# A two-layer hybrid decoder trunk: recurrence levels on 64-column halves, and low halves of 30 weight blocks of each mixer added by a DMA

## The chip, the cores and the metric

The kernel runs on one core of one Trainium2 chip. The metric is device time in microseconds (us) of one execution; the kernel before took 2127.11 us, the median of 3 runs (2126.46 to 2127.39). A profile is one execution with the hardware profiler on. Its engines: PE is TensorE's matmul side and PEld its weight load, DVE is VectorE, ACT is ScalarE, POOL is GpSimd, SP is SyncE, which here only issues DMAs.

## What is computed

Two layers, each with a half-step gated feed-forward, a mixer, and a second feed-forward; 512 tokens, width 1024, all in float32. The change lies in the mixer's gated linear recurrence (4 heads, 128 x 128 state, chunks of 64 tokens in the reference) and in how the mixer's weights are prepared.

```python
for l in range(DEPTH):
    h = rms_norm(x, gn[0])
    x = x + 0.5 * rms_norm(swiglu(h, w_ffn1_gate[l], w_ffn1_up[l], w_ffn1_down[l]), gn[1])
    h = rms_norm(x, gn[2])
    proj = h @ w_in[l]
    hq, hf, hi, hg, aq, ak, av, gate_a, gate_b = jnp.split(proj, IN_SPLITS, axis=-1)
    y_hg = hgrn2_mixer(hq, hf, hi, hg, lb_all[l], hgrn_head_gain[l]) @ w_branch_hgrn[l]
    y_at = swa_sink_attention(aq, ak, av, attn_sinks[l]) @ w_branch_attn[l]
    mixed = jax.nn.sigmoid(gate_a) * y_hg + jax.nn.sigmoid(gate_b) * y_at
    x = x + rms_norm(mixed @ w_out[l], gn[3])
    h = rms_norm(x, gn[4])
    x = x + 0.5 * rms_norm(swiglu(h, w_ffn2_gate[l], w_ffn2_up[l], w_ffn2_down[l]), gn[5])
...
# in hgrn2_mixer, per chunk
G = jnp.cumsum(gb, axis=2)
diff = G[:, :, :, None, :] - G[:, :, None, :, :]
decay = jnp.exp(jnp.where(causal[:, :, None], diff, -jnp.inf))
scores = jnp.einsum('bhtd,bhtsd,bhsd->bhts', qb, decay, kb)
o = o_inter + jnp.einsum('bhts,bhse->bhte', scores, vb)
```

A score of the recurrence between a query t and an earlier key s is the sum over d of q[t,d], k[s,d] and the product of the forget gates f between them. The kernel needs those scores for the whole sequence of 512 tokens.

## The kernel before

**Weights.** Every large product is made of three products of float32r halves: high by high, high by low, low by high. A `Stream` brings the weights in blocks of 128 x 1024 through four buffers `w`, issued on SP's queue. `Stream.split` makes a block's halves: ScalarE casts the block to `whi` (L321), and then one of two ways makes `wlo`. For kind "u" VectorE subtracts (L328). For kinds "v", "a" and "d" ScalarE writes the negated rounded block to `wlo` (L325) and a DMA issued on POOL's queue adds the block into it (L326). Six slots hold `whi` and `wlo`; blocks are split three ahead of the one in use, and as far as the slots allow. A slot is free when TensorE has used the block, 24 products of 512 columns.

**Order on TensorE.** The program writes TensorE's order out by hand. `mm` adds each product's estimated time to a clock, `order.t`. Coroutines (recurrence heads, attention blocks) run in steps; each step ends with a `yield` of a time after which the next is due, taken from the table WAIT. After each block of a weight product `order.poll` runs the steps that are due, so their products are put between the large ones. The other engines' order is chosen by the framework.

**Recurrence scores** (`recurrence_scores`, once for each of 4 heads in each of 2 layers). `kz`, `q`, `f` are 128 x 512: the head's 128 channels by 512 tokens, four tiles of 128 tokens. The levels b = 1, 2, 4, 8, 16, 32, 64 join neighbouring blocks of b tokens to blocks of 2b. At each level the odd block's queries times the even block's keys give scores, with `qa` and `kz` having been multiplied by running products of f (`meet`, L976 to L988). Levels come in pairs (1, 2), (4, 8), (16, 32), the last, 64, alone. For a pair a tile `mv` of 4 x 192 columns is packed: 64 query columns of level b, 64 of level 2b, and 64 of level 2b times a product of f (L995 to L1000). Four fp32 products (one for each tile of 128 tokens, all 128 keys as weights) write two PSUM banks `aux`. Each has columns for keys that don't belong; `place` copies under a mask (L972) those that do into `sd`, 128 x 4 x 128. Before the levels, the diagonal is computed as four products of 128 columns into `p0` and multiplied by the identity (L949), which also writes zeros into the rest of `sd`.

Three banks are called `aux`, five `acc`. The steps of a head before: head (waits 2600 on the planner's clock), diagonal (0), then for each pair: pack (4000), products and placing (1720), then last level, and products between tiles. The first two heads of a layer are spawned together, the other two later.

Attention has a product of the same shape as the ones the change makes: its output products (`po` in `attend`) use 64 weight columns and write partitions 0 to 63 or 64 to 127 of one bank, by turns. Its score products use 64 partitions as the contracted side.

Of the kernel before, what the change touches and what calls it, by code (L numbers as in the profile page):

```python
# [7 lines left out]
F32 = mybir.dt.float32  # L8
F32R = mybir.dt.float32r
I32 = mybir.dt.int32  # L10
# [5 lines left out]
P = 128  # L16
# [13 lines left out]
SLOTS = 61  # L30

WAIT = dict(
    early=0.0, first=0.0, spread=2300.0, squares=1700.0, lay=34500.0, laid=770.0, normed=7600.0, final=2600.0,
    head=2600.0, diag=0.0, level=1720.0, chunks=1270.0, blocks=350.0, norm=2370.0, gate=8000.0,
    values=1200.0, scores=2000.0, exp=9000.0, shares=4500.0, turn=1900.0, turned=3000.0, rest=1200.0, lent=3500.0, apart=4000.0, block=2000.0, pair=4000.0, att0=1260.0, att1=12300.0,
)
W32, WS, AHEAD, TAIL, PLAIN, FIRST, EARLY, LATE = 4, 6, 3, 4, 4, 7, 4, 8
# [8 lines left out]
def trunk(ctx: ExitStack, tc: tile.TileContext, xin, wall, gains, lbT, hgain, sinks, c_dist, c_mask, c_ident, out):  # L46
# [12 lines left out]
    def nm(s):  # L59
        seq[0] += 1  # L60
        return f"{s}_{seq[0]}"
# [10 lines left out]
    def aux():  # L72
        return ps.tile([P, S], F32, tag="aux", name=nm("aux"), bufs=3)
# [40 lines left out]
    def mm(o, lhsT, rhs, start, stop):  # L114
        nc.tensor.matmul(o, lhsT, rhs, start=start, stop=stop)  # L115
# [822 lines left out]
    def recurrence_scores(q, f, kz, box):  # L938
# [15 lines left out]
        prod, off = f, 0  # L954

# [3 lines left out]
            return v[:, :, 0, :], v[:, :, 1, :]  # L959

        def odd(t, b):
            return t.rearrange("p (c n two b) -> p c n two b", c=TT, two=2, b=b)[:, :, :, 1, :]

        def dense(t, b):
            return t.rearrange("p c (n b) -> p c n b", b=b)

        def spread(v, b):
            return v.to_broadcast([P, v.shape[1], b])

        def place(b, m, src, c):  # L970

            nc.vector.copy_predicated(  # L972
                sd.rearrange("p c (n two b) -> p c n two b", two=2, b=b)[:, c, :, 1, :],
                mask[:, m, :].rearrange("p (n b) -> p n b", b=b).unsqueeze(1).to_broadcast([P, 2, 64 // b, b]),
                dense(src, b),
            )  # L976

        def meet(b):

# [11 lines left out]
        for i, b in enumerate(LEVELS[:-1:2]):  # L991


            mv = sb.tile([P, TT, 192], F32, tag="tt", name=nm("mv"), bufs=2)
            nc.scalar.copy(dense(mv[:, :, :64], b), odd(qa, b))  # L995
            first = meet(b)
            next(first)
            nc.scalar.copy(dense(mv[:, :, 64:128], 2 * b), odd(qa, 2 * b))
            way = prod.rearrange("p (c n four) -> p c n four", c=TT, four=4)[:, :, :, 1:2]
            nc.vector.tensor_tensor(  # L1000
                dense(mv[:, :, 128:], 2 * b), odd(qa, 2 * b), way.to_broadcast([P, TT, P // (4 * b), 2 * b]), op=ALU.mult
            )
# [24 lines left out]

        s1 = big(F32, [P, 2, P])
# [241 lines left out]
    for l in range(DEPTH):  # L1270
        for n in (0, 2, 4):
            if n == 2:
                ws.plain(2 * H + 6 + 8 + LATE * 3 // 2)
                for _ in range(KT - LATE // 2):
                    ws.gates()
                ws.rows(KT, False)
            else:
                p = FIRST if l + n == 0 else PLAIN
                ws.plain(min(2 * p, 8))
                ws.plain(max(2 * p - 8, 0), "v")  # L1280
                ws.pairs(FT - p)
                ws.rows(FT, True)
# [151 lines left out]
```

## Time and profile before

| what | value |
|---|---|
| median of 3 runs | 2127.11 us |
| span of the profiled execution | 2123.9 us |
| TensorE products | 13293 records |
| granted TensorE clock | 0.999 |
| HBM read, written | 213.58 MB, 14.73 MB |

The mixers run from about 380 to 700 us and from about 1430 to 1750 us; feed-forwards fill the rest. The table of stages below has, for each engine, busy us and in brackets the number of instructions, then the granted clock, the share of time that the DMA engines were busy, and the rate. Its first two rows are the first mixer, its first 200 us with the recurrence and attention and the rest with the branches; the third is the recurrence part of the second mixer.

```profile
core 0: us, PE busy (x) PEld busy (x) DVE busy (x) ACT busy (x) POOL busy (x), PEclk, DMA share, GB/s
380.00:580.00 200.00, 198.40 (x1081) 163.54 (x1080) 148.34 (x389) 96.94 (x205) 0.00 (x0) 1.00 0.21 69
580.00:700.00 120.00, 120.00 (x691) 106.26 (x690) 82.97 (x120) 56.24 (x81) 6.90 (x8) 1.00 0.51 146
1430.00:1640.00 210.00, 208.40 (x1130) 171.91 (x1129) 155.30 (x401) 101.05 (x211) 0.86 (x1) 1.00 0.22 71
```

How to read the rest. A timeline row is: start in us, length in us, engine, line, operation, output<-input, shape, number of instructions merged, and in brackets idle time of the engine just before and what ended it. Products are pipelined, so a product's length is longer than its distance to the next. "128*64 128x512" is 128 contracted rows, 64 weight columns, 512 moving columns. An fp32 product is two records. A row of a view that groups instructions ends with busy us, mean ns of one, idle time of the engine before them and what ended it. Almost all products carry the line of the helper `mm` (L115); they are told apart by their tiles (`mv`, `s`, `whi`, `wlo`) and shapes. A row of waits gives us in total, how many, and the longest. A row of DMA issues gives count, KB each and the median us from issue to landing.

### The profile page before, as it was taken

To read this page: it belongs to the slowest core of one execution; us is meant where nothing else is said; L and a number is where in the kernel's file an instruction comes from. 1 tells how busy PE (TensorE), PEld (TensorE's weight loads), DVE (VectorE), ACT (ScalarE), POOL (GpSimd) and SP (SyncE) were. 2 spreads that over 40 slices of the span, in tenths; PEclk is the share of its full clock that TensorE was granted. 3 is DMA by queue.
4 is the path that set the end of the run, shared out by engine and by line. 5 is a ranking of instruction groups with operands and counts; after the bars stand their busy time and mean duration, and the time that the engine had idled before them with its cause. 6 is when DMAs were issued, how large, how long until landed. Compare 5 with 4: busy or idle time off the path is not lost.

```text
span 2123.9 us, 34765 instructions
## 1 busy us (share of the span) xinstructions
PE 2110.6 (99%) x13293; PEld 1898.1 (89%) x13293; DVE 1573.4 (74%) x2793; ACT 1119.0 (53%) x1884; POOL 152.2 (7%) x180
## 2 busy tenths in 40 slices
PE   9999999999999999999999999999999999999998
PEld 8899988887888999998899998898778989999987
DVE  5877886768776777789587778767687757777884
ACT  7555555346445555556455556453554545555562
POOL 0011000000000011110001110000000000111000
PEclk9999999999999999999999999999999999999999
DMA  8677663221236357774447775632122463677751
GB/s 251 149 185 182 167 181 118 92 67 64 66 100 208 120 125 176 182 197 123 153 113 177 183 183 141 197 119 80 60 70 60 124 194 110 149 180 182 185 158 51
DMA packets 146870, 298.48 MB, mean 141 GB/s; under 512 B 15664, under 2 KB 73488, under 8 KB 146704
## 3 DMA queue, kind: packets, MB, share of 16 engines
q1 hardware_dynamic: 121216, 228.31, 32.7%
q0 software_dynamic: 25344, 67.91, 18.6%
q8 instruction: 104, 1.70, 0.3%
q14 instruction: 62, 0.51, 0.1%
q10 hardware_dynamic: 144, 0.05, 0.0%
HBM read 213.58 MB, written 14.73 MB: 107 GB/s over the span
## 4 chain that ended last, share of the span: by engine, by line
PE 75%; DVE 7%; ACT 3%; issue 1%; DMA 1%; SPq 0%; ACTq 0%; DVEq 0%
PE acc L115 55%; PE aux L115 19%; DVE s L398 1%; PE aux L122 1%; ACT whi L321 1%; DVE wlo L283 1%; DMA w<-wall 1%; DVE wlo L328 1%; PE acc L122 1%; ACT s L397 1%; DVE tt L265 0%; DVE w L264 0%; DVE s L273 0%; DVE w L274 0%; ACT whi L278 0%
## 5 line engine op out<-in xcount | busy, mean ns | idle before, releaser
L115 PE MATMUL acc<-s,whi 128*128 128x256 f32 (+1 forms) x4968 | 1068.8, 312 | 0.7 <-DVE s L901 0.7
L115 PEld LDWEIGHTS acc<-s,whi 128*128 128x128 f32 x4968 | 810.1, 191 | 48.7 <-issue 3.7
L115 PE MATMUL acc<-s,wlo 128*128 128x256 f32 (+1 forms) x2484 | 770.2, 310 | 0.1
L115 PEld LDWEIGHTS acc<-s,wlo 128*128 128x128 f32 x2484 | 474.1, 191 | 26.0 <-DVE wlo L328 0.4
L321 ACT CAST whi<-w 128x1024 fp32r<-128x1024 f32 (+1 forms) x341 | 316.6, 947 | 242.0 <-PE aux L115 100.2
L115 PE MATMUL acc<-whi,s 128*128 128x512 f32 x1264 | 414.5, 394 | 0.0
L321 ACT CAST whi<-tt 128x1024 fp32r<-128x1024 f32 x154 | 161.4, 1048 | 337.7 <-DVE tt L315 199.5
L328 DVE TENSOR_TENSOR wlo<-w,whi 128x1024 fp32r<-128x1024 f32 (+1 forms) x181 | 218.5, 1216 | 135.3 <-ACT whi L321 131.6
L115 PEld LDWEIGHTS acc<-whi,s 128*128 128x128 f32 x1264 | 237.1, 188 | 55.7 <-issue 3.2
L328 DVE TENSOR_TENSOR wlo<-tt,whi 128x1024 fp32r<-128x1024 f32 x154 | 188.1, 1222 | 101.6 <-ACT whi L321 101.6
L326 POOL DMA_DIRECT2D wlo<-w x160 | 138.2, 865 | 1723.5 <-ACT wlo L325 1363.1
L115 PE MATMUL acc<-wlo,s 128*128 128x512 f32 x632 | 246.7, 390 | 1.2 <-DVE wlo L283 1.2
L115 PE MATMUL aux<-s,whi 128*128 128x256 f32 x1232 | 225.1, 283 | 0.0
L115 PE MATMUL aux<-whi,s 128*128 128x512 f32 x592 | 196.7, 390 | 0.0
L115 PEld LDWEIGHTS aux<-s,whi 128*128 128x128 f32 x1232 | 192.2, 192 | 0.0
L115 PE MATMUL aux<-s,wlo 128*128 128x256 f32 x616 | 174.3, 283 | 0.0
L115 PEld LDWEIGHTS acc<-wlo,s 128*128 128x128 f32 x632 | 118.8, 188 | 25.5 <-DVE wlo L283 2.4
L115 PEld LDWEIGHTS aux<-whi,s 128*128 128x128 f32 x592 | 111.2, 188 | 22.9
L325 ACT ACTIVATE wlo<-w 128x1024 fp32r<-128x1024 f32 (+1 forms) x160 | 129.8, 844 | 0.0
L397 ACT CAST s<-s 128x512 fp32r<-128x512 f32 (+1 forms) x164 | 88.4, 580 | 75.8 <-DVE s L456 72.2
L115 PEld LDWEIGHTS aux<-s,wlo 128*128 128x128 f32 x616 | 118.3, 192 | 0.0
L115 PE MATMUL aux<-wlo,s 128*128 128x512 f32 x296 | 115.2, 389 | 0.0
(182 smaller groups left out, 2189.1 us busy)
## 6 DMA issues: line engine op xcount, KB each, us to landing
w<-wall SPq DMA_DIRECT2D x267, 512.0 KB, 3.7
wlo<-w POOLq DMA_DIRECT2D x83, 512.0 KB, 5.5
w<-wall SPq DMA_DIRECT2D x288, 128.0 KB, 3.4
wlo<-w POOLq DMA_DIRECT2D x77, 256.0 KB, 3.3
x_d<-s SPq DMA_DIRECT2D x48, 256.0 KB, 2.1
s<-x_d SPq DMA_DIRECT2D x48, 256.0 KB, 5.5
w<-wall SPq DMA_DIRECT2D x34, 256.0 KB, 3.2
s<-wall SPq DMA_DIRECT2D x64, 128.0 KB, 3.7
```

What stands on the lines that cost most here:

```text
L115: nc.tensor.matmul(o, lhsT, rhs, start=start, stop=stop)
L122: nc.tensor.transpose(o, src, ident)
L283: nc.vector.tensor_tensor(it.lo[:, h[c]], w[c], it.hi[:, h[c]].bitcast(F32), op=ALU.subtract)
L321: i = nc.scalar.copy(it.hi[:, c], w[:, c])
L325: nc.scalar.mul(it.lo[:, c], w[:, c], -1.0)
L326: nc.gpsimd.dma_start(it.lo[:, c].bitcast(F32), w[:, c], accum_op=ALU.add)
L328: nc.vector.tensor_tensor(it.lo[:, c], w[:, c], it.hi[:, c].bitcast(F32), op=ALU.subtract)
L397: nc.scalar.copy(hi, src)
L398: nc.vector.tensor_tensor(lo, src, hi.bitcast(F32), op=ALU.subtract)
```

## The change

In the recurrence, each tile of 128 tokens is taken as two halves of 64. `mv` has 96 columns for each half instead of 192 for each tile; a product uses 64 weight columns (that half's keys) and writes partitions 0 to 63 for the lower half and 64 to 127 for the upper, by turns, all four tiles into one `aux` bank in place of two. The diagonal is computed in the same way, in the step of the first pair and into a bank of its own, one step later than before; its step and wait are gone. `place` works on 64 partitions and all four tiles, so a pair still has six masked copies, of 128 columns each. The last level uses the lower half's keys alone and is copied by ScalarE without a mask. POOL clears the part of `sd` below that. The planner's clock counts an fp32 product of 64 weight columns at half.

In the stream, 30 of the 34 plain blocks of each mixer become kind "v" instead of "u": their low halves are made by ScalarE and the adding DMA, not by VectorE. The mask loses its last entry and half of its columns, and is loaded by two DMAs.

```diff
@@ mm
-        order.t += max(n / 2.4, 27.0) * 4 if rhs.dtype == F32 else max(n / 2.4, 107.0)
+        if rhs.dtype == F32:
+            order.t += max(n / 2.4, 27.0) * (2 if lhsT.shape[1] == 64 and n < 256 else 4)
+        else:
+            order.t += max(n / 2.4, 107.0)
@@ recurrence_scores
         sd = big(F32, [P, TT, P])
-        p0 = aux()
-        for c in range(TT):
-            cs = slice(c * P, (c + 1) * P)
-            mm(p0[:, cs], kz[:, cs], q[:, cs], True, True)
-        nc.vector.tensor_tensor(
-            sd, p0.rearrange("p (c t) -> p c t", c=TT), ident.unsqueeze(1).to_broadcast([P, TT, P]), op=ALU.mult
-        )
-        yield WAIT["diag"]
+        nc.gpsimd.memset(sd[64:, :, :64], 0.0)
...
-        def place(b, m, src, c):
-
-            nc.vector.copy_predicated(
-                sd.rearrange("p c (n two b) -> p c n two b", two=2, b=b)[:, c, :, 1, :],
-                mask[:, m, :].rearrange("p (n b) -> p n b", b=b).unsqueeze(1).to_broadcast([P, 2, 64 // b, b]),
-                dense(src, b),
-            )
+        def place(b, m, lv, g):
+
+            for h in range(2):
+                r = slice(64 * h, 64 * h + 64)
+                nc.vector.copy_predicated(
+                    sd[r].rearrange("p c (x n two b) -> p c x n two b", x=2, two=2, b=b)[:, :, h, :, 1, :],
+                    mask[r, m, :].rearrange("p (n b) -> p n b", b=b).unsqueeze(1).to_broadcast([64, TT, 32 // b, b]),
+                    dense(lv[r, :, g * 32 : g * 32 + 32], b),
+                )
...
-            mv = sb.tile([P, TT, 192], F32, tag="tt", name=nm("mv"), bufs=2)
-            nc.scalar.copy(dense(mv[:, :, :64], b), odd(qa, b))
+            mv = sb.tile([P, 2 * TT, 96], F32, tag="tt", name=nm("mv"), bufs=2)
+            nc.scalar.copy(dense(mv[:, :, :32], b), odd(qa, b))
...
             yield WAIT["pair"]
-            lv = [aux()[:, :384].rearrange("p (c t) -> p c t", c=2) for _ in range(2)]
+            p0 = None if i else aux()
+            lv = aux()[:, : TT * 96].rearrange("p (c t) -> p c t", t=96)
             for c in range(TT):
-                mm(lv[c // 2][:, c % 2, :], kz[:, c * P : (c + 1) * P], mv[:, c, :], True, True)
+                for h in range(2):
+                    r, x = slice(64 * h, 64 * h + 64), 2 * c + h
+                    if not i:
+                        mm(p0[r, x // 2 * 64 : x // 2 * 64 + 64], kz[:, x * 64 : x * 64 + 64], q[:, x * 64 : x * 64 + 64], True, True)
+                for h in range(2):
+                    r, x = slice(64 * h, 64 * h + 64), 2 * c + h
+                    mm(lv[r, c, :], kz[:, x * 64 : x * 64 + 64], mv[:, x, :], True, True)
             next(first, None)
             for _ in meet(2 * b):
                 pass
-            for j, v in enumerate(lv):
-                c = slice(2 * j, 2 * j + 2)
-                place(b, 3 * i, v[:, :, :64], c)
-                place(2 * b, 3 * i + 1, v[:, :, 64:128], c)
-                place(2 * b, 3 * i + 2, v[:, :, 128:], c)
+            if i == 0:
+                for h in range(2):
+                    r = slice(64 * h, 64 * h + 64)
+                    nc.vector.tensor_tensor(
+                        sd[r, :, r], p0[r, : TT * 64].rearrange("p (c t) -> p c t", c=TT),
+                        ident[r, r].unsqueeze(1).to_broadcast([64, TT, 64]), op=ALU.mult,
+                    )
+            place(b, 3 * i, lv, 0)
+            place(2 * b, 3 * i + 1, lv, 1)
+            place(2 * b, 3 * i + 2, lv, 2)
             yield WAIT["level"]
         b = LEVELS[-1]
         lv = aux()
         for c in range(TT):
-            mm(lv[:, c * b : (c + 1) * b], kz[:, c * P : (c + 1) * P], qa[:, c * P + b : (c + 1) * P], True, True)
+            mm(lv[:b, c * b : (c + 1) * b], kz[:, c * P : c * P + b], qa[:, c * P + b : (c + 1) * P], True, True)
         for _ in meet(b):
             pass
-        v = lv[:, :256].rearrange("p (c t) -> p c t", c=TT)
-        for j in range(2):
-            c = slice(2 * j, 2 * j + 2)
-            place(b, len(MASKS) - 1, v[:, c, :], c)
+        nc.scalar.copy(sd[:b, :, b:], lv[:b, : TT * b].rearrange("p (c t) -> p c t", c=TT))
         yield WAIT["level"]
@@ the stream's items, for each layer
             if n == 2:
-                ws.plain(2 * H + 6 + 8 + LATE * 3 // 2)
+                ws.plain(4)
+                ws.plain(2 * H + 2 + 8 + LATE * 3 // 2, "v")
@@ constants
-    mask = const([P, len(MASKS), 64], "mask", I32)
-    nc.sync.dma_start(mask, c_mask)
+    mask = const([P, len(MASKS) - 1, 32], "mask", I32)
+    for h in range(2):
+        nc.sync.dma_start(mask[64 * h : 64 * h + 64], c_mask[64 * h : 64 * h + 64, :-1, 32 * h : 32 * h + 32])
```

More of the change, by code (lines that the diff above doesn't have):

```diff
@@ L32 @@
 WAIT = dict(
-    early=0.0, first=0.0, spread=2300.0, squares=1700.0, lay=34500.0, laid=770.0, normed=7600.0, final=2600.0,
-    head=2600.0, diag=0.0, level=1720.0, chunks=1270.0, blocks=350.0, norm=2370.0, gate=8000.0,
+    first=0.0, spread=2300.0, squares=1700.0, lay=34500.0, laid=770.0, normed=7600.0, final=2600.0,
+    head=2600.0, level=1720.0, chunks=1270.0, blocks=350.0, norm=2370.0, gate=8000.0,
     values=1200.0, scores=2000.0, exp=9000.0, shares=4500.0, turn=1900.0, turned=3000.0, rest=1200.0, lent=3500.0, apart=4000.0, block=2000.0, pair=4000.0, att0=1260.0, att1=12300.0,
@@ L961, in odd @@
         def odd(t, b):
[L962 removed]
+            return t.rearrange("p (x n two b) -> p x n two b", x=2 * TT, two=2, b=b)[:, :, :, 1, :]
         def dense(t, b):
[L965 removed]
+            return t.rearrange("p x (n b) -> p x n b", b=b)
         def spread(v, b):
             return v.to_broadcast([P, v.shape[1], b])
[L970 to L976 removed]
+        def place(b, m, lv, g):
[6 more added lines that the diff above has]
+                )
         def meet(b):
@@ L991, in recurrence_scores @@
         for i, b in enumerate(LEVELS[:-1:2]):
-            mv = sb.tile([P, TT, 192], F32, tag="tt", name=nm("mv"), bufs=2)
-            nc.scalar.copy(dense(mv[:, :, :64], b), odd(qa, b))
+            mv = sb.tile([P, 2 * TT, 96], F32, tag="tt", name=nm("mv"), bufs=2)
+            nc.scalar.copy(dense(mv[:, :, :32], b), odd(qa, b))
             first = meet(b)
             next(first)
-            nc.scalar.copy(dense(mv[:, :, 64:128], 2 * b), odd(qa, 2 * b))
-            way = prod.rearrange("p (c n four) -> p c n four", c=TT, four=4)[:, :, :, 1:2]
+            nc.scalar.copy(dense(mv[:, :, 32:64], 2 * b), odd(qa, 2 * b))
+            way = prod.rearrange("p (x n four) -> p x n four", x=2 * TT, four=4)[:, :, :, 1:2]
             nc.vector.tensor_tensor(
-                dense(mv[:, :, 128:], 2 * b), odd(qa, 2 * b), way.to_broadcast([P, TT, P // (4 * b), 2 * b]), op=ALU.mult
+                dense(mv[:, :, 64:96], 2 * b), odd(qa, 2 * b), way.to_broadcast([P, 2 * TT, 16 // b, 2 * b]), op=ALU.mult
             )
             yield WAIT["pair"]
-            lv = [aux()[:, :384].rearrange("p (c t) -> p c t", c=2) for _ in range(2)]
+            p0 = None if i else aux()
+            lv = aux()[:, : TT * 96].rearrange("p (c t) -> p c t", t=96)
             for c in range(TT):
-                mm(lv[c // 2][:, c % 2, :], kz[:, c * P : (c + 1) * P], mv[:, c, :], True, True)
+                for h in range(2):
[5 more added lines that the diff above has]
+                    mm(lv[r, c, :], kz[:, x * 64 : x * 64 + 64], mv[:, x, :], True, True)
             next(first, None)
```

## The prediction

> **What bounds the kernel now.** I read the page's busy times first, then TensorE's waits, then timelines of TensorE around each group that the change touches.
>
> ```profile
> span 2123.9 us, 34765 instructions
> PE 2110.6 (99%) x13293; PEld 1898.1 (89%) x13293; DVE 1573.4 (74%) x2793; ACT 1119.0 (53%) x1884; POOL 152.2 (7%) x180
> ```
> ```profile
> PE aux L115 <- DVE s L972: 3.2, 2, 1.6
> ```
>
> A busy TensorE proves little, because its ends are modelled; but its waits are short too, and in the changed code it waits only twice, 3.2 us in all. So the time is a sum of TensorE start-to-start distances, and a group of products is priced by what it adds between two starts.
>
> ```profile
> 386.43 0.39 PE L115 MATMUL acc<-s,wlo 128*128 128x512 f32 x1
> ...
> 387.11 0.39 PE L115 MATMUL acc<-s,wlo 128*128 128x512 f32 x1
> 387.34 1.05 PE L115 MATMUL aux<-s,s 128*128 128x128 f32 x8
> ...
> 388.69 0.39 PE L115 MATMUL acc<-s,wlo 128*128 128x512 f32 x1
> 408.39 0.39 PE L115 MATMUL acc<-s,wlo 128*128 128x512 f32 x1
> 408.62 1.46 PE L115 MATMUL aux<-mv,s 128*128 128x192 f32 x8
> ...
> 410.39 0.40 PE L115 MATMUL acc<-s,wlo 128*128 128x512 f32 x1
> 423.93 0.40 PE L115 MATMUL acc<-s,wlo 128*128 128x512 f32 x1
> 424.16 1.00 PE L115 MATMUL aux<-s,s 128*128 128x64 f32 x8
> ...
> 425.51 0.40 PE L115 MATMUL acc<-s,wlo 128*128 128x512 f32 x1
> ```
>
> From one wlo start to the next stand three ordinary products (the wlo one and two whi ones): 387.11 - 386.43 = 0.68 us. Anything over 0.68 is the group's between them. The diagonal (p0 of one head) costs 388.69 - 387.11 - 0.68 = 0.90, one pair of levels 2.00 - 0.68 = 1.32, the last level 1.58 - 0.68 = 0.90. An fp32 product is two records, so each group has eight. A record of 192 columns takes 1.32 / 8 = 0.165 us, one of 128 and one of 64 columns both 0.11: under 128 columns the moving side no longer decides. A head costs 0.90 + 3 x 1.32 + 0.90 = 5.76 us.
>
> **TensorE's part of the change.** Products with 64 weight columns, two side by side in the halves of one bank, exist already, in attention:
>
> ```profile
> 466.86 0.39 PE L115 MATMUL acc<-wlo,s 128*128 128x512 f32 x1
> ...
> 467.41 1.08 PE L115 MATMUL aux<-s,s 128*64 128x512 f32 x4
> ...
> 468.75 0.39 PE L115 MATMUL acc<-wlo,s 128*128 128x512 f32 x1
> 510.40 0.40 PE L115 MATMUL acc<-s,wlo 128*128 128x512 f32 x1
> 510.73 1.94 PE L115 MATMUL aux<-s,s 128*64 128x512 f32 x8
> ...
> 513.16 0.40 PE L115 MATMUL acc<-s,wlo 128*128 128x512 f32 x1
> ```
> ```profile
> 510.72 0.20 PEld L115 LDWEIGHTS aux<-s,s 128*64 128x64 f32 x4 [0.37 <-ACT s L397]
> L115 PEld LDWEIGHTS aux<-s,s 128*64 128x64 f32 x56 | 3.3, 135 | 6.3 <-issue 4.9 <-ACT s L397 0.7 <-DVE s L988 0.7
> L115 PEld LDWEIGHTS aux<-mv,s 128*128 128x128 f32 x192 | 32.4, 189 | 5.7 <-issue 3.7
> ```
>
> Four records cost 1.89 - 0.68 = 1.21 us, eight 2.76 - 0.68 = 2.08. The four more cost 0.87, so two side by side take 0.43 us. A single 512-column record at the rate above would take 512 x 0.165 / 192 = 0.44: **the halves overlap fully**. What remains, 1.21 - 0.87 = 0.34 to 0.36, is a fixed price for each such group; I use 0.36. The fp32 groups with whole weights have none: 8 x 0.11 is already 0.88 of 0.90.
>
> For short records the load of weights matters. Four loads of 64 columns, 135 ns each, fill 0.20 us together, so all four began within 0.065: each half can load its next weights some 0.055 us after the last, half of the 0.11 above. Loads of 64 columns also last 54 ns less than those of 128 (135 against 189). So for two side by side I take 0.084 us at 96 columns (half of 0.165, rounded up) and 0.058 at 64 columns (the load, with a little over).
>
> - First pair with the diagonal: 8 x (0.084 + 0.058) + 0.36 = 1.50, before 0.90 + 1.32 = 2.22: 0.72 saved.
> - The two other pairs: 8 x 0.084 + 0.36 = 1.03 each, before 1.32: 0.58 saved.
> - Last level: all four products use the lower half alone, so nothing runs side by side: 8 x 0.058 + 0.36 = 0.82, before 0.90: 0.08 saved. If load and product don't overlap within one half it is 8 x 0.11 + 0.36 = 1.24: 0.34 lost. I take the former: in the row of 64 columns before, a load of 0.11 and a product hide in 0.11.
>
> Sum: 1.38 us a head, 8 heads, **11.0 us**. Bounds: with the last level at 1.24, 1.38 - 0.42 = 0.96 a head, 7.7; with a fixed price of only 0.20 (a bubble of 0.1 us on each side, as from 510.40 + 0.23 to 510.73), four groups gain 0.64 more, 16.1.
>
> **VectorE's and the other engines' part.**
>
> ```profile
> L972 DVE COPY_PREDICATED s<-mask,aux 128x128 f32<-128x128 int32 x160 | 47.7, 344 | 7.0 <-PE aux L115 6.9
> L328 DVE TENSOR_TENSOR wlo<-w,whi 128x1024 fp32r<-128x1024 f32 x179 | 217.2, 1222 | 135.3 <-ACT whi L321 131.6 <-PE aux L115 1.6 <-DMA w<-wall 1.3
> L325 ACT ACTIVATE wlo<-w 128x1024 fp32r<-128x1024 f32 x83 | 86.8, 1046 | 0.0
> L326 POOL DMA_DIRECT2D wlo<-w x160 | 138.2, 865 | 1723.5 <-ACT wlo L325 1363.1 <-DVE wlo L328 106.7 <-DVE s L461 105.2
> wlo<-w POOLq DMA_DIRECT2D x83, 512.0 KB, 5.5
> ```
>
> Placing keeps its width in columns (128 elements on 64 partitions), so 18 copies a head in place of 20; the diagonal's one operation becomes two of half the columns. That is nearly even and runs beside TensorE's products: nothing. The last level's placing becomes one ScalarE copy, which the output products read several groups later: nothing.
>
> The 60 moved blocks take 60 x 1.222 = 73 us off VectorE, put 60 x 1.046 = 63 on ScalarE and 60 x 0.865 = 52 on POOL, and add 60 transfers. All of it hides behind products. The low half is ready after the cast, 1.05 + 0.87 + 5.5 = 7.4 us, and blocks are split three ahead of use, each used for 24 products: 3 x 24 x 0.227 = 16 us. Without that cover each block would stop TensorE for up to 7.4 us. The raw buffer is held those 5 us longer; four of them at 5.4 us a block still leave the load its time. On POOL an issue now waits for ScalarE's negated copy, which waits for a slot that TensorE frees; behind it stand only later blocks' issues and the clears of sd (one a head), which wait for nothing but a free tile, and for a clear nobody waits before the output products. The mask's second load is one more issue on SP's queue at the start, ahead of weights that are split three blocks before use: nothing.
>
> **The two waits.**
>
> ```profile
> 399.10 0.39 PE L115 MATMUL acc<-s,wlo 128*128 128x512 f32 x1
> 399.33 0.81 PE L115 MATMUL aux<-mv,s 128*128 128x192 f32 x4
> 401.74 0.89 PE L115 MATMUL aux<-mv,s 128*128 128x192 f32 x4 [1.60 <-DVE s L972]
> ...
> 402.94 0.39 PE L115 MATMUL acc<-s,wlo 128*128 128x512 f32 x1
> ```
> ```profile
> 392.73 0.75 DVE L1000 TENSOR_TENSOR mv<-s,s 128x256 f32<-128x256 f32 x2
> 393.41 1.22 DVE L328 TENSOR_TENSOR wlo<-w,whi 128x1024 fp32r<-128x1024 f32 x1
> 397.05 1.23 DVE L328 TENSOR_TENSOR wlo<-w,whi 128x1024 fp32r<-128x1024 f32 x1 [2.42 <-ACT whi L321]
> ```
>
> In each mixer the second head's first pair stops for 3.84 - 0.68 - 1.32 = 1.84 us, since the first head holds two of three aux banks until VectorE, stuck behind low halves, places them. Afterwards VectorE is free there, but the first pair still takes two banks (p0 and lv), freed only after about eight short operations. And a step is gone: the first pair now comes 4.0 us of the planner's time after the point of 387.1, some 392 us, while its operands were ready at 393.5. So this term lies between -3.7 (both waits gone) and +2.8 (1.4 us more in each mixer). I take 0.
>
> Sum: span 2123.9 - 11.0 = 2112.9. The median of the runs, 2127.1, lies 3.2 above the profiled span, so I forecast **2116 us**.
>
> **The rivals.**
>
> *A floor under each pair of records.* Attention's scores, two products side by side by rows, show one:
>
> ```profile
> 434.18 0.39 PE L115 MATMUL acc<-wlo,s 128*128 128x512 f32 x1
> 434.73 0.89 PE L115 MATMUL aux<-s,s 64*128 64x128 f32 x12
> ...
> 435.89 0.39 PE L115 MATMUL acc<-wlo,s 128*128 128x512 f32 x1
> ```
>
> Six pairs cost 1.71 - 0.68 - 0.36 = 0.67, 0.11 each, for 128 columns in one pass. If that is the rate of issue and not the load of 128 weight columns, pairs of 96 and 64 columns take 0.11 too: 2.12 + 2 x 1.24 + 1.24 = 5.84 a head, 0.08 worse: 2128. Against it stand the four loads begun within 0.065 us. [...] Chance 7%.
>
> *New waits eat the gain.* Scores, turns and levels were timed for the old lengths; two or three waits of 1 to 2 us in each mixer take 4 to 8 us: 2120 to 2124. The trace's spare time speaks against more than that. Chance 18%, a third of it above 2123.
>
> *The waits vanish and the switch is cheaper:* 2127.1 - 11.0 - 3.7 or less, 2107 to 2112. Chance 13%.
>
> *Slower: ScalarE makes the pairs late.* Its copies feed every pair's moving operand, and now stand behind twice the weight work.
>
> ```profile
> 389.57 1.04 ACT L321 CAST whi<-w 128x1024 fp32r<-128x1024 f32 x1 [2.80 <-PE acc L115]
> 390.53 0.42 ACT L995 COPY mv<-s 128x256 f32<-128x256 f32 x1
> 406.59 0.40 ACT L998 COPY mv<-s 128x256 f32<-128x256 f32 x1
> ```
>
> At 390.5 the copy already stood behind a cast. If each of the 24 pairs waited for one more operation of 1.05 us, that is 25 us: 2127 - 11 + 25 = 2141. It decides from 11.0 / 24 = 0.46 us a pair. Against it: the copy that ended at 407.0 was not used before 408.6, and a group may slip 1.6 us unseen. Chance 10%.
>
> **How the numbers follow.** Forecast (2112 to 2120) 52%, better 13%, part eaten 18%, floor 7%, slower 10%. A change under 0.2%, 4.3 us, can't be told from none: that is 2122.9 to 2131.4. Faster: 52 + 13 + 12 = 77%; within: 6 + 7 = 13%; slower 10%. The range 2109 to 2126 takes in the bound 7.7 with its waits at +2.8 (2122), most of the better case, and stops short of floor and slower.
>
> **What would show it.** Groups of 64 weight columns with 96 moving columns that add 1.0 us between two wlo starts, the first pair 1.5, the last level 0.8; loads of two halves that begin together; no wait of TensorE on wlo. It is wrong if such a group adds 1.25 or more, if starts of the two halves lie 0.08 us apart, or if TensorE waits for mv or sd in most groups.

## The result, and the profile after

| kernel | median, us | lowest to highest | profiled span, us |
|---|---|---|---|
| before (12 runs) | 2126.99 | 2126.29 to 2128.21 | 2123.9 |
| after (12 runs) | 2126.10 | 2124.45 to 2128.17 | 2124.2 |

After against before is 0.9995, with a 95% interval of 0.9988 to 1.0002: no difference that can be told. The forecast was 2116 us, and 2126.1 lies 0.1 us above the upper end of its range, 2109 to 2126.

The page after, busy us by engine:

```profile
PE 2103.5 (99%) x13549; PEld 1874.7 (88%) x13549; DVE 1522.8 (72%) x2725; ACT 1176.7 (55%) x1952; POOL 206.5 (10%) x248
```

VectorE has 50.6 us less to do, ScalarE 57.7 and POOL 54.3 more; TensorE is 7.1 us less busy in a span that is as long. So it waits more. Of TensorE's waits after, these are the ones that before does not have, two of 0.2 us aside (us in total, how often, the longest):

```profile
PE aux L115 <- ACT mv L996: 4.0, 2, 2.0
PE aux L115 <- DVE s L1042: 1.6, 2, 0.9
PE aux L115 <- DVE s L984: 1.3, 2, 0.7
PE aux L115 <- DVE s L1018: 1.2, 2, 0.6
PE aux L115 <- DMA wlo<-w: 1.1, 1, 1.1
PE acc L125 <- DVE s L741: 0.6, 2, 0.3
```

Before, the mixers had one row of waits, 3.2 us. Now there are five, each once in each mixer, 8.7 us together, and a DMA that is in neither mixer.

The timeline of TensorE after shows both things side by side, the groups that run freely and those that wait:

```profile
392.12 0.39 PE L115 MATMUL acc<-s,wlo 128*128 128x512 f32 x1
...
392.60 0.34 PE L115 MATMUL aux<-mv,s 128*64 128x96 f32 x4
392.77 0.28 PE L115 MATMUL aux<-s,s 128*64 128x64 f32 x4
392.88 0.34 PE L115 MATMUL aux<-mv,s 128*64 128x96 f32 x4
...
394.29 0.39 PE L115 MATMUL acc<-s,wlo 128*128 128x512 f32 x1
...
394.98 0.39 PE L115 MATMUL acc<-s,wlo 128*128 128x512 f32 x1
...
396.25 0.39 PE L115 MATMUL aux<-mv,s 128*64 128x96 f32 x4 [0.62 <-DVE s L1018]
...
397.98 0.39 PE L115 MATMUL acc<-s,wlo 128*128 128x512 f32 x1
...
403.44 0.39 PE L115 MATMUL acc<-s,wlo 128*128 128x512 f32 x1
405.83 0.88 PE L115 MATMUL aux<-mv,s 128*64 128x96 f32 x16 [2.00 <-ACT mv L996]
...
407.22 0.40 PE L115 MATMUL acc<-s,wlo 128*128 128x512 f32 x1
...
407.93 0.39 PE L115 MATMUL acc<-s,wlo 128*128 128x512 f32 x1
408.24 0.88 PE L115 MATMUL aux<-mv,s 128*64 128x96 f32 x16
...
409.62 0.40 PE L115 MATMUL acc<-s,wlo 128*128 128x512 f32 x1
...
419.89 0.39 PE L115 MATMUL acc<-s,wlo 128*128 128x512 f32 x1
...
421.38 0.40 PE L115 MATMUL acc<-s,wlo 128*128 128x512 f32 x1
...
543.38 0.39 PE L115 MATMUL acc<-s,wlo 128*128 128x512 f32 x1
544.43 0.65 PE L115 MATMUL aux<-s,s 128*64 128x64 f32 x8 [0.66 <-DVE s L984]
...
545.58 0.39 PE L115 MATMUL acc<-s,wlo 128*128 128x512 f32 x1
```

Read by the prediction's rule (from one wlo start to the next, less 0.68 us), the free groups cost: first pair with the diagonal 394.29 - 392.12 - 0.68 = 1.49 us, another pair 409.62 - 407.93 - 0.68 = 1.01, last level 421.38 - 419.89 - 0.68 = 0.81. A head is 1.49 + 2 x 1.01 + 0.81 = 4.32 us for 5.76 before; eight heads give **11.5 us**. The same rule gives what the others waited beyond these prices: the second head's first pair 3.00 - 0.68 - 1.49 = 0.83, the first head's second pair 3.78 - 0.68 - 1.01 = 2.09, a later last level 2.20 - 0.68 - 0.81 = 0.71. With 0.55 at the turn (the transposition of the normalized activations with which a mixer begins, 366.8 us), 0.77 at attention's output products (501.3) and 1.11 at the products between tiles (550.5), all found in the same way, and a last 0.12, one mixer waits 6.2 us where it had waited 1.84. Two mixers: **8.6 us** given back.

The rest went outside the mixers. The timeline of three engines after, near 940 us (feed-forward):

```profile
926.60 1.57 ACT L328 ACTIVATE wlo<-w 128x512 fp32r<-128x512 f32 x2
927.52 1.81 POOL L329 DMA_DIRECT2D wlo<-w  x2 [8.39 <-ACT wlo L328]
...
936.80 0.63 ACT L328 ACTIVATE wlo<-w 128x512 fp32r<-128x512 f32 x1
939.68 0.86 POOL L329 DMA_DIRECT2D wlo<-w  x1 [10.35 <-ACT s L400]
...
943.89 0.39 PE L115 MATMUL aux<-s,wlo 128*128 128x256 f32 x1 [1.07 <-DMA wlo<-w]
```

One of two merged ScalarE copies is 0.63 long, so the first ended at 927.23 and its DMA was issued 0.29 later, as almost all are. The one at 936.80 ended at 937.43, and its DMA was issued 2.25 later; TensorE had to wait for the block. (The profile puts this wait of POOL down to a cast of activations, `s`, which belongs to another block's work: the trace shows no cause for the delay.)

To see in which stage each kernel gains, the span is cut at the start of the same four weight products in every kernel (us; the columns other than before and after are the experiments below):

| stage | before | after | e1 | e2 | e4 | e6 | e8 | e11 | e12 |
|---|---|---|---|---|---|---|---|---|---|
| to the first mixer | 358.4 | 358.1 | 358.1 | 358.4 | 358.4 | 357.8 | 358.4 | 357.8 | 358.0 |
| first mixer | 341.6 | 340.4 | 341.2 | 341.9 | 338.5 | 336.7 | 336.2 | 335.5 | 369.7 |
| feed-forwards between | 709.9 | 712.3 | 709.3 | 712.6 | 711.9 | 709.9 | 711.5 | 709.8 | 710.0 |
| second mixer | 340.2 | 339.0 | 338.6 | 340.4 | 337.2 | 335.3 | 334.8 | 334.0 | 368.6 |
| last feed-forward | 373.7 | 374.4 | 374.4 | 374.8 | 374.4 | 374.2 | 374.2 | 374.3 | 374.5 |

After against before: the mixers -2.5 (that is -11.5 and +8.6, within 0.4), the feed-forwards between +2.4, the last +0.6, the start -0.3: nothing in all. Followed product by product, 1.2 of the +2.4 come at the wait at 943 us. Another 0.6, near 1303 us, stand at the same place in e10 below, whose feed-forwards are those of before (its stage between the mixers takes 710.9 us): they are not the change's.

### The profile page after: what moved, and what is told of

Its sections match the earlier page's. It is cut to its first block, busy times and chain, and to the rows that moved or that the text cites. A ratio compares the mean times of both kernels' runs of the same rounds, so it can differ in the third digit from the quotient of the medians.

```text
span 2124.2 us, 35436 instructions
## 1 busy us (share of the span) xinstructions
PE 2103.5 (99%) x13549; PEld 1874.7 (88%) x13549; DVE 1522.8 (72%) x2725; ACT 1176.7 (55%) x1952; POOL 206.5 (10%) x248
## 4 chain that ended last, share of the span: by engine, by line
PE 79%; DVE 10%; ACT 6%; issue 2%; DMA 2%; SPq 0%; ACTq 0%; DVEq 0%; POOLq 0%
PE acc L115 58%; PE aux L115 19%; ACT whi L324 2%; DMA w<-wall 1%; DVE s L401 1%; PE aux L125 1%; ACT wlo L328 1%; DVE wlo L286 1%; ACT s L400 1%; DVE s L970 1%; DVE wlo L331 1%; PE acc L125 1%; ACT whi L281 1%; DVE tt L268 0%; DVE w L267 0%
## 5 line engine op out<-in xcount | busy, mean ns | idle before, releaser
L329 POOL DMA_DIRECT2D wlo<-w x220 | 189.9, 864 | 1669.0 <-ACT wlo L328 1290.7
L331 DVE TENSOR_TENSOR wlo<-w,whi 128x1024 fp32r<-128x1024 f32 (+1 forms) x121 | 145.4, 1212 | 107.5 <-ACT whi L324 104.4
L328 ACT ACTIVATE wlo<-w 128x1024 fp32r<-128x1024 f32 x220 | 193.3, 903 | 16.6 <-PE acc L115 16.6
```

What stands on the lines that cost most here:

```text
L328: nc.scalar.mul(it.lo[:, c], w[:, c], -1.0)
L329: nc.gpsimd.dma_start(it.lo[:, c].bitcast(F32), w[:, c], accum_op=ALU.add)
L331: nc.vector.tensor_tensor(it.lo[:, c], w[:, c], it.hi[:, c].bitcast(F32), op=ALU.subtract)
```

## The experiments

The theory after this reading: the shorter groups are worth what was forecast; TensorE's order, written out by hand, brings it to each next group earlier, and VectorE's chain, which did not get shorter, now ends each wait; the moved blocks cost a little of their own. The rivals: the halves cost TensorE time elsewhere; the moved blocks alone ate the gain; or VectorE is slower for a reason that better due times can't mend. All ratios below are against the kernel before, timed again beside each set of runs (medians 2126.69 to 2126.79), with their 95% intervals.

**The two parts apart.** e1_rec_only is the kernel after without the moved blocks; e2_dma_only is the kernel before with them.

```diff
@@ e1_rec_only, against after
-                ws.plain(2 * H + 2 + 8 + LATE * 3 // 2, "v")
+                ws.plain(2 * H + 2 + 8 + LATE * 3 // 2)
@@ e2_dma_only, against before
-                ws.plain(2 * H + 6 + 8 + LATE * 3 // 2)
+                ws.plain(4)
+                ws.plain(2 * H + 2 + 8 + LATE * 3 // 2, "v")
```

> The recurrence part alone: all 34 plain blocks of a mixer keep their low halves on VectorE. In the changed kernel the groups on TensorE cost what was forecast (about 11.3 us less in all), but new waits of 4.3 us more in each mixer stand against it. Theory 'order' (TensorE's order was timed for the old lengths and now reaches groups before VectorE's chain is ready): VectorE has 73 us more to do here, so its chain is later still and waits grow; 2126 to 2132. Theory 'ScalarE' (the doubled weight work on ScalarE makes the waits): waits fall back to the old 3.7 us, so 2127 - 11 = 2116.

> The weight part alone: the recurrence as before, 30 blocks of each mixer by the adding DMA. Theory 'order': VectorE is freed where the two waits of 1.84 us stood, so 2123 to 2127. Theory 'ScalarE': 4 us of new waits in each mixer, 2130 to 2135.

e1: 2123.13 us, 0.9984 (0.9975 to 0.9992). e2: 2129.64 us, 1.0014 (1.0005 to 1.0023). The parts give -3.7 and +2.9, and their sum, -0.8, is the whole change. Both fall between the ranges of their two theories. So the halves alone don't bring 11 us either, and the moved blocks are not free. In e1, whose VectorE does all low halves, the second pair waits longer than in the kernel after (4.6 us in the two mixers, for 4.0). Its two mixers are no shorter (679.8 us, for 679.4): it is faster in the feed-forwards. The moved blocks do relieve VectorE there, and bring waits of their own elsewhere: e2's mixers are no shorter than before's, and its feed-forwards between are 2.7 us longer.

**Later due times.** e3_later is the kernel after with later steps (in ns of the planner's clock): level, after a pair's placing, 1720 to 4220; chunks, before the products between tiles, 1270 to 2770; turned, after attention's last turn, 3000 to 4500.

> The changed kernel with three due times made later on the planner's clock: after a pair's placing 4.2 us in place of 1.72, before the products between tiles 2.77 in place of 1.27, after the last turn of attention 4.5 in place of 3.0. Nothing else changes. Theory 'order': most of the 6 us of waits in each mixer go, and the time falls by 5 to 9 us, to 2117 to 2121. Theory 'VectorE's chain is the bound itself' (the end of the recurrence is what the mixer's end waits for): the time doesn't fall, since the waits only move to the end of the mixer; 2125 to 2130.

e3: 2122.25 us, 0.9978 (0.9969 to 0.9987), between the two ranges. 3.9 us come back of more than 8: the second pair still waits 1.3 us in each mixer, the second head's first pair 0.6. The wait is not a matter of due times alone.

**The order of the masked copies.** e4_half_by_half is the kernel after with a pair's three copies of the lower half first, then the three of the upper one. The copies are the same.

```diff
@@ e4_half_by_half, against after
-            place(b, 3 * i, lv, 0)
-            place(2 * b, 3 * i + 1, lv, 1)
-            place(2 * b, 3 * i + 2, lv, 2)
+            for h in range(2):
+                place(b, 3 * i, lv, 0, h)
+                place(2 * b, 3 * i + 1, lv, 1, h)
+                place(2 * b, 3 * i + 2, lv, 2, h)
```

> The changed kernel with the six masked copies of a pair sorted: three on the lower 64 partitions, then three on the upper, in place of lower and upper by turns. In the changed kernel they start 0.47 us apart in the first pair, before 0.285. If the change of partitions between neighbours makes them slow, four of six distances fall to about 0.3, the chain of the first pair of two heads gets 1.4 us shorter and the wait before the second pair falls from 2.1 to below 1: 2123 to 2125. If each masked copy on 64 partitions is slow in itself, or the copies wait for each other, distances stay 0.47 and the time 2126.

e4: 2120.89 us, 0.9974 (0.9965 to 0.9983), 5.2 us faster than the kernel after by the medians (4.5 by the two ratios), and faster than the 2123 to 2125 expected. The wait at the second pair is gone; its group starts 0.42 after the wlo product of 403.71, where a free one starts 0.31 after (408.24 - 407.93):

```profile
404.13 0.88 PE L115 MATMUL aux<-mv,s 128*64 128x96 f32 x16
```

Order alone, with the same work, took 2 us out of each mixer's longest wait. VectorE's timeline after, at that place, and one row of before (six masked copies each):

```profile
395.24 0.87 DVE L1018 TENSOR_TENSOR s<-aux,ident 64x256 f32<-64x256 f32 x2
396.13 2.81 DVE L970 COPY_PREDICATED s<-mask,aux 64x128 f32<-64x128 int32 x6
...
405.27 0.76 DVE L998 TENSOR_TENSOR mv<-s,s 128x256 f32<-128x256 f32 x2
```
```profile
403.55 1.90 DVE L972 COPY_PREDICATED s<-mask,aux 128x128 f32<-128x128 int32 x6
```

Six copies by turns on lower and upper partitions take 2.81 us, six on all partitions 1.90, though one copy lasts as long as before, by the row of its group after (344 ns in the prediction's row):

```profile
L970 DVE COPY_PREDICATED s<-mask,aux 64x128 f32<-64x128 int32 x144 | 49.6, 345 | 3.7
```

The difference is in their distances: by turns they start (2.81 - 0.44) / 5 = 0.47 us apart, with the 0.44 that such a copy lasts in e6's rows below, so of two neighbours the second starts when the first has ended. For two heads that is some 1.8 us. So the placing of the first two heads held the work on the next pairs' `mv` back until 404 to 406 us, and TensorE, there at 403.7, waited.

The distances are the smaller part of what e4 wins. From the first diagonal operation to the last product into `mv`, VectorE does the same 25 operations in 10.3 us there and in 10.7 in the kernel after: operations on all partitions, which begin at partition 0, now stand between upper copies, and don't overlap with them (0.45 to 0.49 from start to start). The larger part is the sequence that came with the new order. In e4 the product into the first head's `mv` (L998) no longer stands behind the second head's last two copies and a product of forget gates:

```profile
403.56 0.42 DVE L998 TENSOR_TENSOR mv<-s,s 128x256 f32<-128x256 f32 x1
404.01 0.45 DVE L970 COPY_PREDICATED s<-mask,aux 64x128 f32<-64x128 int32 x1
404.49 0.42 DVE L982 TENSOR_TENSOR s<-s,s 128x256 f32<-128x256 f32 x1
404.95 0.46 DVE L970 COPY_PREDICATED s<-mask,aux 64x128 f32<-64x128 int32 x1
```

It starts 8.1 us after the first diagonal operation, where the kernel after needs 10.0 (405.27 - 395.24). Three operations fewer ahead of it, at 0.47, 0.47 and 0.34, are 1.3 of these 2.0 us.

**Both together, and with due times.** e5_half_u is e4 without the moved blocks. e6_half_u_due is e5 with level 2720, chunks 2770, and the diagonal's two VectorE operations ahead of the second `meet` (the products of forget gates). e8_e6_with_dma is e6 with the 30 moved blocks of each mixer. e9_due_alone is e1 with e6's due times; e10_before_due is the kernel before with them.

> The changed kernel with the masked copies sorted by halves (as in e4_half_by_half) and all low halves of plain blocks on VectorE (as in e1_rec_only). Theory 'additive' (the weight part costs about 2.9 us by itself, mostly in the feed-forwards, and the recurrence part is independent of it): 2120.9 - 2.9 = 2118, 2116 to 2119.5. Theory 'VectorE needs the relief' (the sorted copies gain only because VectorE is free of 30 low halves): the wait before the second pair comes back at 2 to 3 us in each mixer, and the time is 2122 to 2124.

> As e5_half_u, with two due times later on the planner's clock (after a pair's placing 2.72 in place of 1.72, before the products between tiles 2.77 in place of 1.27) and the diagonal's two operations on VectorE ahead of the products of forget gates. Theory 'order': the waits left in the recurrence (0.85 at the second head's first pair, 0.5 at the last level, 1.3 at the products between tiles, in each mixer) shrink to under 1 us together, 2113 to 2116, the forecast of the whole change at last. Rival: the waits move to other places, no change against e5_half_u.

> As e6_half_u_due, but with 30 blocks of each mixer by the adding DMA as in the change. In e2_dma_only that part cost 2.9 us, of which 0.5 in each mixer (the turn at its start) and about 2 in the feed-forwards (the 114th adding DMA left POOL 2.0 us late just where it is needed). Theory 'the cost lies outside the recurrence': the same 2 to 3.5 us again, 2117.5 to 2119. Rival 'VectorE needs the relief': the waits left in the recurrence (2.4 us in each mixer) go and pay for it, 2115 to 2116.5.

> As e1_rec_only (halves by turns, low halves on VectorE), with e6's two later due times and nothing else of e6. Theory 'order': most of e6's gain over e5 is the due times, so waits of 6.9 and 5.6 us in the two mixers fall to 3 to 4 each: 2117 to 2119. Rival 'VectorE's chain': the slow masked copies by turns hold the second pair anyway, 2120 to 2123.

> The kernel before with the same two later due times. It has only two waits of 1.84 us to lose, at the second head's first pair, which these due times don't move. Theory 'order is a matter of the new lengths': no change, 2125 to 2128. Rival 'any later order is better': 2120 to 2124.

| kernel | median, us | ratio | interval |
|---|---|---|---|
| e5 (order of copies) | 2121.50 | 0.9975 | 0.9965 to 0.9985 |
| e6 (e5, due times, diagonal first) | 2115.68 | 0.9950 | 0.9937 to 0.9962 |
| e8 (e6, moved blocks) | 2117.01 | 0.9955 | 0.9943 to 0.9968 |
| e9 (e1, due times) | 2120.98 | 0.9974 | 0.9964 to 0.9984 |
| e10 (before, due times) | 2127.12 | 1.0002 | 0.9993 to 1.0011 |

The due times do nothing for the kernel before and 2.1 us for the halves: they don't speed anything up, they only stop TensorE from coming to a group too early. They don't do it alone either (e9 keeps 4.7 us of waits for mv), and nor does the order of copies: against e1 it adds 1.6 us (e5). e6, with both and with the diagonal first, stands 7.4 us ahead of e1 and 11 ahead of before, though TensorE's rows leave 1.9 us of waits in each mixer, where under 1 was expected. What the diagonal's place adds was not run by itself.

e5 lies between the ranges of its two theories: the second pair waits 0.5 us in each mixer, not the 2 to 3 of 'VectorE needs the relief', and the moved blocks, which e5 lacks and e4 has, are worth almost nothing there (2121.50 and 2120.89). e8 is 0.5 us faster than the first of its ranges. Once TensorE no longer waits in the mixers, the moved blocks shorten these by another 0.5 us each and lengthen the feed-forwards by 1.6 (the table of stages): on balance 1.3 us slower, less than the 2.9 of e2 and within the two intervals.

**Where the moved blocks cost.** e7_two_more_dma is e4 with two more moved blocks in each mixer, so that whatever hangs on the count of adding DMAs falls on another block.

```diff
@@ e7_two_more_dma, against e4
-                ws.plain(4)
-                ws.plain(2 * H + 2 + 8 + LATE * 3 // 2, "v")
+                ws.plain(2)
+                ws.plain(2 * H + 4 + 8 + LATE * 3 // 2, "v")
```

> As e4_half_by_half, with 32 blocks of each mixer by the adding DMA in place of 30. In each trace so far the 114th adding DMA leaves POOL 2.0 us late, wherever it falls: at 1235 us before, at 940 us in the three kernels with 30 blocks by DMA, where TensorE then waits 1.2 to 1.9 us for it. Theory 'the 114th': two more such DMAs in the first mixer put the late one two issues earlier, where low halves are some 10 us ahead of use; the wait at 940 us vanishes, 2119 to 2120. Rival 'the place' (the start of the seven products at the end of a feed-forward is late in itself when low halves come by DMA): the wait stays, and the time 2121.

e7: 2121.19 us, 0.9974 (0.9965 to 0.9984). The late issue moved with the count, from 938.0 us in e4 to 928.2:

```profile
925.31 1.57 ACT L328 ACTIVATE wlo<-w 128x512 fp32r<-128x512 f32 x2
928.19 1.76 POOL L329 DMA_DIRECT2D wlo<-w  x2 [10.35 <-ACT s L864]
```

The first of the two copies ended at 925.94, 2.25 before its DMA. There TensorE does not wait for it, and no wait for an adding DMA is left in e7's waits. Counted over POOL's queue it is the 114th DMA in before, after, e2, e7 and e11 alike (of the adding DMAs alone, which the expectation counts, the 106th in before and e11 and the 110th in the others); before has it at 1235.3 us, where nobody waits. The total did not fall, because the turn of each mixer now waits 1.1 us instead of 0.3 (the row for L741: 2.3 us in two): against e4 the feed-forwards between are 2.1 us shorter and the mixers together 1.5 longer.

**The best version.** e11_later_yet is e6 with level at 3720.

> As e6_half_u_due, with the due time after a pair's placing at 3.72 in place of 2.72. Waits left in e6: 0.64 at the second pair, 1.33 at the first products between tiles and 0.46 at the output products, in each mixer. Theory 'order': the first two go, 2112 to 2114. Rival: waits move into attention or to the end of the recurrence, as in e3_later, 2115 to 2118.

e11: 2113.20 us, 0.9939 (0.9926 to 0.9951), 13.5 us faster than before and the fastest here. Of the waits listed above none for `mv`, for the diagonal or for a level is left; each mixer keeps one of 0.9 us at attention. By the spans it gains 2123.9 - 2111.4 = 12.5 us: the 11.5 of the groups, and one of what before had waited.

**Half partitions by themselves.** e12_halves_alone changes nothing but VectorE: the kernel before, with each masked copy, and the product that fills the last 64 columns of `mv`, written as two operations, lower and upper 64 partitions.

```diff
@@ e12_halves_alone, against before (the product for mv in the same way)
-            nc.vector.copy_predicated(
...
+            for h in range(2):
+                r = slice(64 * h, 64 * h + 64)
+                nc.vector.copy_predicated(
+                    sd[r].rearrange("p c (n two b) -> p c n two b", two=2, b=b)[:, c, :, 1, :],
...
```

> The kernel before, with each masked copy and the product that fills the last 64 columns of mv written as two operations, one on the lower and one on the upper 64 partitions (twice the operations, the same elements, the same results). In the kernel before, neighbouring 128-partition masked copies of 128 elements start 0.198 or 0.283 us apart and are 0.29 to 0.48 long; the products of 256 elements start 0.335 apart and are 0.42 long. Theory, half-partition neighbours do not overlap on VectorE: the two halves of a product start 0.42 to 0.45 apart, and copies start at least their own length apart, 0.29 to 0.47. Rival, the lost overlap in the changed kernel came from its order of copies or from its bank: the two halves of a product start 0.335 apart and the copies 0.2 to 0.29 apart, as on 128 partitions. Either way VectorE has some 30 us more to do, and TensorE waits longer than 3.7 us in the mixers: a span of 2125 to 2145.

e12: 2182.49 us in its one run, beside 2125.48 for the kernel before. VectorE's timeline:

```profile
392.27 1.73 DVE L1004 TENSOR_TENSOR mv<-s,s 64x256 f32<-64x256 f32 x4
...
400.23 5.12 DVE L974 COPY_PREDICATED s<-mask,aux 64x128 f32<-64x128 int32 x11
```

Four products end 1.73 us after the first starts; one lasts 0.42, so they start (1.73 - 0.42) / 3 = 0.44 apart, where those of before on 128 partitions start 0.335 apart. Eleven copies start (5.12 - 0.44) / 10 = 0.47 apart. Neither the order of the changed kernel nor its banks are in e12, so the halves by turns are enough to lose the overlap. My span of 2125 to 2145 was far too low: both mixers became 28 us longer, with TensorE waiting for VectorE (17.2 us for the masked copies alone, by its waits) and at a lower clock (last section).

These 57 us are not the price of the turns alone, because e12 also doubles the number of operations. VectorE's busy time grew by 81.5 us, where I had expected some 30. Its masked copies:

```profile
L974 DVE COPY_PREDICATED s<-mask,aux 64x128 f32<-64x128 int32 x320 | 108.5, 339 | 9.3 <-PE aux L115 1.1
```

Before, 160 took 47.7 us (the prediction's row of L972), 0.298 each with their overlap. By that, as an estimate, 320 would take 95 us, and the lost overlap is 13 of the 61 us more.

Whether it is the width or the turns, e6's timeline tells. By the program's order the masked copies (L970) there are three lower, then three upper, those of L1015 lower and upper, and operations with 128 rows begin at partition 0:

```profile
395.06 0.44 DVE L970 COPY_PREDICATED s<-mask,aux 64x128 f32<-64x128 int32 x1
395.31 0.44 DVE L986 TENSOR_TENSOR s<-s 128x256 f32<-128x256 f32 x1
395.68 0.43 DVE L970 COPY_PREDICATED s<-mask,aux 64x128 f32<-64x128 int32 x1
395.91 0.45 DVE L1015 TENSOR_TENSOR s<-aux,ident 64x256 f32<-64x256 f32 x1
396.28 0.89 DVE L970 COPY_PREDICATED s<-mask,aux 64x128 f32<-64x128 int32 x2
396.97 0.45 DVE L1015 TENSOR_TENSOR s<-aux,ident 64x256 f32<-64x256 f32 x1
397.34 0.43 DVE L970 COPY_PREDICATED s<-mask,aux 64x128 f32<-64x128 int32 x1
397.81 0.43 DVE L984 TENSOR_TENSOR s<-s,s 128x256 f32<-128x256 f32 x1
```

From a lower copy to an operation on all partitions 0.25, back to a lower copy 0.37, on to the next head's lower diagonal 0.23, to the third lower copy 0.37: all overlap. The two merged at 396.28, third lower and first upper, end 0.89 after the first starts: 0.44 apart, no overlap. Then upper to upper diagonal 0.25 and upper copy 0.37 again, and from that to an operation at partition 0, 0.47. So not the width: in these rows the overlap is lost with **a change of the first partition** between two neighbours, from 0 to 64 or back (0.44 and 0.47 apart, for 0.23 to 0.37 where it stays).

Nor is it that one operation waits for the other's semaphore. By the trace's records most copies by turns do have such a wait, but the first upper copy here (at 396.72) and the second half of the second product in e12 (at 393.58) have none, and still start 0.01 us after the end of their neighbour.

## Why the prediction was wrong

*TensorE's part* was right in every term: 1.50, 1.03 and 0.82 us forecast for 1.49, 1.01 and 0.81, and 11.0 for 11.5 in all. The loads of two halves bear out the 0.084 and 0.058 a pair: in the timeline after, four records of 96 columns take 392.77 - 392.60 = 0.17 and four of 64 take 392.88 - 392.77 = 0.11. The floor of the first rival, 0.11 us for each pair of records, is refuted by the same rows: 0.085 and 0.055.

*"The two waits … I take 0"* is the step that failed. Its bounds, -3.7 to +2.8, looked at one wait in each mixer, the one that before showed. Measured, the waits of the mixers grew by 8.6 us: one wait of 1.84 became seven. The rival "New waits eat the gain" named the mechanism and priced it at 4 to 8, with 18%. What I left out is that TensorE comes sooner to the later groups too, while their producers keep nearly the old pace. Before, the second pair of the first head started at 408.62; now TensorE was ready for it at some 403.7, 4.9 us sooner. Of these, 4.3 are there at the first pair already (the wlo product ahead of it starts at 392.12, before at 396.40), since the diagonal's step and its groups of 0.90 are gone from ahead of it: the prediction saw this, and priced it for that pair alone. Before, the operands were ready by 407.0 (the prediction's row of the ScalarE copy L998), 1.6 ahead of use; now they were ready at 405.8, only 1.2 earlier. 4.9 - 1.6 - 1.2 is the wait of 2.1.

*"Placing … nearly even … nothing"* was wrong in its size and is part of why the operands came so little earlier. I counted elements and operations, and not distances: six copies 2.81 us for 1.90, the diagonal two times 0.44. That neighbours by turns lose their overlap is shown (e12, e6); how much of the 8.6 us it makes is not, since e4 changes VectorE's sequence along with the distances. The diff alone shows that each copy of a pair begins at another partition than the one before it; what that costs I did not weigh. In the traces here neighbours that last 0.42 to 0.46 us and change between partitions 0 and 64 start 0.42 to 0.49 apart (after, e4, e6, e12), those of e6's rows that don't change 0.23 to 0.37.

*"All of it hides behind products"* was too kind to the moved blocks. e2 puts them at +2.9 us (some 0.5 of it, near 1303 us, is in e10 as well): a wait of TensorE for a low half in the feed-forward (1.7 us there, 1.1 in the kernel after, where no wait on wlo was to appear), and 0.55 at each turn, which is there in the kernel after and e2 and absent in e1; e7, with two more of these blocks, has 1.1 us of idle time there for 0.3. That ScalarE's negated copies stand before the turn's own work there is argued, not shown. The sum of 7.4 us for a low half counts the issue twice: the row's 5.5 runs from the issue's start, so an ordinary block takes 1.05 + 0.29 + 5.5 = 6.8 from the start of its copy. The issue that is 2 us late was not in it.

*"Slower: ScalarE makes the pairs late"* did not come: the second pair's wait ends with ScalarE's copy into mv, but that copy in turn had waited for VectorE, and in e1, with ScalarE relieved, the wait is longer. ScalarE's row after:

```profile
405.05 0.74 ACT L996 COPY mv<-s 128x256 f32<-128x256 f32 x2 [3.85 <-DVE s L982]
```

## What to carry to other kernels

When a group on the bounding engine gets shorter under a fixed order, go along its producers from that point on and ask of each group whether its operands come sooner too; if not, the gain turns into waits, and has to be fetched by moving due times and the producers' order (here 2127 to 2113 us instead of 2126). When an operation is split by partitions, sort the pieces so that neighbours begin at the same partition (in e6 0.23 to 0.37 us apart, for 0.44 and 0.47 where it changes between 0 and 64), and look at what else stands ahead of the operation that the bounding engine waits for: here that was the larger part. A part of a change that relieves an engine which isn't the bound should be timed alone: here it cost 2.9 us by itself, and almost nothing beside the sorted copies.

## What the runs showed of the hardware

- VectorE: neighbours that begin at the same partition overlapped by some 0.08 us (products of 256 elements in before: 0.42 long, 0.335 apart) to 0.2 (masked copies among others in e6: 0.44 long, 0.23 to 0.25 apart); where the first partition changes between 0 and 64, the second started 0.01 to 0.04 after the first had ended (after, e4, e6, e12). Not every neighbour that begins at the same partition overlaps: in e6 the lower copies at 395.06, 399.72 and 405.55 start 0.01 to 0.02 after the end of an operation on all partitions; the timeline shows no cause.
- The 114th DMA on POOL's queue is issued 2.25 us after the copy it needs, where 0.29 is usual, in each kernel in which it was counted (before, after, e1, e2, e4, e7, e11, e12), whatever block it carries: at 1235.3 us in before, 939.7 after, 941.6 in e2, 938.0 in e4, 928.2 in e7. So is the 220th where there are so many (after, at 1930.2, e2, e4, e7). Why is open; no run tried another way of issuing.
- In e12 (one run), TensorE's granted clock was lower in the two stages in which it waits most: by the view of stages 0.96 in the first mixer (busy 201.3 of 220 us) and 0.98 in the second (198.5 of 220), for 1.00 in both before (busy 198.4 of 200 and 208.4 of 210; the clock is the column behind the five engines).

```profile
380.00:600.00 220.00, 201.30 (x1036) 161.24 (x1035) 184.72 (x470) 91.30 (x198) 0.00 (x0) 0.96 0.18 59
```
